# Differential attention in an encoder layer: a second plain fp32 quarter of the weights, and GpSimd work tied to VectorE's combinations

## The chip, the cores and the metric

The kernel runs on one core of one Trainium2 chip. The metric is the device time of one execution in microseconds. Three executions of the kernel before took 2710.55, 2710.61 and 2710.95 us; the median is 2710.61 us.

## The reference, cut to what matters

One encoder layer on x of 2048 positions by 1024 channels: RMS norm, an input projection, differential attention (4 heads) beside a gated linear recurrence (512 channels), an output projection, a gated feed-forward part with a short convolution, and a last RMS norm. All is fp32. The change touches the attention alone:

```
sc = einsum(q_block, k) * scale - slope[h] * |i - j|      # two score maps per head, c = 0, 1
p  = softmax(sc)
w  = p[c=0] - lam * p[c=1]                                # 128 queries x 2048 keys
o  = w @ v                                                # 128 queries x 128
o  = rms_norm(o, subln_g) * (1 - lambda_init)             # over the 128 columns
```

## The kernel before, in words

`phase1` makes q, k, v and the recurrence and leaves them in DRAM; `phase2` is the attention; `phase3` starts the output projection; then the feed-forward part runs. fp32 products are made either as one plain fp32 matmul, or by `mm3` (L79) as three fp32r matmuls of a high and a low part of each factor: high x high, high x low, low x high. `split` (L72) makes the parts: the high one is a copy to fp32r on ScalarE, the low one the fp32 difference, on VectorE or GpSimd as `lo_eng` says.

The attention works on 4 heads x 16 tiles of 128 queries, 64 steps, and two neighbouring tiles of a head form a pair. `step(n, cur)` (L550) writes the work of one step out by hand for five tiles at different ages. `manual_schedule` (L613) keeps this order on TensorE, VectorE, ScalarE and GpSimd up to the last of the 64 steps; the ten steps that drain the pipeline (L641) are ordered by the framework's planner. In the order of step n:

- `scores(0)` (L397): 12 fp32r matmuls give 1024 keys of both maps into the two buffers of PSUM tile `sc`; `softmax(1)` of the tile before (L415, ScalarE); `biased(0, 0)` and `biased(1, 0)` (L411, VectorE) add the position term and keep the running minimum. They empty `sc`, so `scores(1)` follows them.
- `transposed(0)` and `(1)` of the tile two steps back: 8 transposes of the weights on TensorE, and a copy of each four to SBUF on ScalarE (L442). Quarter 0 goes to `wTn`, plain fp32 for the value product; quarter 1 goes to `wf` and is split by `parts(1)`: high on ScalarE, low on GpSimd (L77, 128x512).
- `parts(2)` of the tile three steps back: the last two quarters (`wg`), high on ScalarE, low on GpSimd (128x1024).
- `values` (L460), two quarters of the product of the pair that is four steps old: in an even step quarters 0 and 1, in an odd one 2 and 3. Quarter 0 is 4 plain fp32 products (L465), each other quarter 12 matmuls of `mm3`. After quarter 3, ScalarE copies the product to `o` (L472) and GpSimd squares it (`osq`, L474).
- `ratio` and `combine(0)` of the tile before (L419 to L427, VectorE): `e0 += rc * e1` on 1024 keys, all in SBUF. The last small instruction of `ratio` (`rc`, L423) also reads two SBUF tensors.
- `scores(1)`, `biased(0, 1)`, `biased(1, 1)`, `transposed(2)` and `(3)`, `softmax(0)`, the second quarter of `values`, `combine(1)`.
- In even steps also the norm of older pairs: `norm_sums` on TensorE, `norm_scale` (VectorE `se`, then GpSimd `rr` and two rows `rb`), two steps later `norm_spread` on TensorE and `scaled` on VectorE (L500).

`sum_values` (L375) adds the two parts of v on GpSimd for the plain quarters, once per head. In the last head, after the odd steps 55, 57, 59 and 61 of 0 to 63, `load_out` (L512) splits a block of the output weights, `wo`: high on ScalarE, low on GpSimd (128x1024), each behind what the step has put on that engine.

Of the kernel before, what the change touches and what calls it, by code (L numbers as in the profile page):

```python
# [9 lines left out]
F32 = mybir.dt.float32  # L10
# [3 lines left out]
AF = mybir.ActivationFunctionType  # L14
ALU = mybir.AluOpType
# [3 lines left out]
P = 128  # L19
# [10 lines left out]
EPS = 1e-6  # L30
# [13 lines left out]
def encoder_layer(ctx, tc, x, w_qkr, w_v, w_out, w_up, w_down, w_a, w_x, par, lams, g_attn, g_ffn, g_fin, out):  # L44
    nc = tc.nc
    V, A, G, T = nc.vector, nc.scalar, nc.gpsimd, nc.tensor

    def pool_of(name, **kw):
        return tc.tile_pool(name=name, reuse_waits="tile", **kw)
# [17 lines left out]
    mhalf = const.tile([P, 4], F32, name="mhalf")  # L67
# [4 lines left out]
    def split(hi, lo, src, hi_eng=A, lo_eng=V):  # L72
        if hi_eng is A:
            A.activation(out=hi, in_=src, func=AF.Copy)  # L74
        else:
            hi_eng.tensor_copy(hi, src)
        lo_eng.tensor_tensor(out=lo, in0=src, in1=hi, op=ALU.subtract)  # L77

    def mm3(ps, lh, ll, rh, rl, first, last):  # L79
        T.matmul(ps, lh, rh, start=first, stop=False)  # L80
        T.matmul(ps, lh, rl, start=False, stop=False)  # L81
        T.matmul(ps, ll, rh, start=False, stop=last)  # L82
# [243 lines left out]
    def phase2(kp):  # L326
        es = ExitStack()
        hip = es.enter_context(pool_of("ah", bufs=2))
        sm = es.enter_context(pool_of("asm", bufs=3))
# [3 lines left out]
        tp_ = es.enter_context(pool_of("at", bufs=2))  # L333
# [4 lines left out]
        ps_t = es.enter_context(pool_of("ps_t", bufs=2, space=PSUM))  # L338
        ps_v = es.enter_context(pool_of("ps_v", bufs=1, space=PSUM))
        PQ = 2 * P  # L340
        NQ = 1

        ones = cp.tile([P, P], F32, name="ones")
        V.memset(ones, 1.0)
# [14 lines left out]
                        op0=ALU.mult)  # L359
# [15 lines left out]
        def sum_values(vs):  # L375
            vn = vp.tile([P, 4 * NQ, P], F32, name="vn", tag="vn")
            G.tensor_tensor(out=vn, in0=vs[0][:, 0:4 * NQ, :].bitcast(F32), in1=vs[1][:, 0:4 * NQ, :].bitcast(F32), op=ALU.add)
            vs.append(vn)
# [9 lines left out]
        class Tile:  # L388
# [35 lines left out]

            def combine(self, hf):
                e0, e1 = [e[:, hf * 1024:(hf + 1) * 1024] for e in self.e]
                V.scalar_tensor_tensor(out=e0, in0=e1, scalar=self.rc, in1=e0, op0=ALU.mult, op1=ALU.add)  # L427

            def transposed(self, i):

                tp = ps_t.tile([P, 4, P], F32, name="tp", tag="tp")
                for m in range(4):
                    T.transpose(tp[:, m, :], self.e[0][:, (4 * i + m) * P:(4 * i + m + 1) * P], ident)  # L433
                if i == 0:
                    dst = self.pair.wn[:, :, self.t % 2 * P:(self.t % 2 + 1) * P]
                elif i == 1:
                    dst = self.wf = tp_.tile([P, 4, P], F32, name="wf", tag="wf", bufs=1)
                else:
                    if i == 2:
                        self.wg = tp_.tile([P, 8, P], F32, name="wg", tag="wg")  # L440
                    dst = self.wg[:, (i - 2) * 4:(i - 1) * 4, :]
                A.activation(out=dst, in_=tp, func=AF.Copy)  # L442

            def parts(self, i):

                j = self.t % 2
                dst = (slice(None), slice(0, 4) if i == 1 else slice(4, 12), slice(j * P, (j + 1) * P))
                split(self.pair.wh[dst], self.pair.wl[dst], self.wf if i == 1 else self.wg, lo_eng=G)

        class Pair:  # L450


            def __init__(self, h, u, vs):
                self.h, self.u, self.vs = h, u, vs
                self.s0 = sm.tile([P, 2], F32, name="s0", tag="s0", bufs=8)
                self.wn = hip.tile([P, 4 * NQ, PQ], F32, name="wTn", tag="wTn")
                self.wh = hip.tile([P, NT - 4 * NQ, PQ], F32R, name="wTh", tag="wTh")
                self.wl = lop.tile([P, NT - 4 * NQ, PQ], F32R, name="wTl", tag="wTl")

            def values(self, part):  # L460
                if part == 0:
                    self.pv = ps_v.tile([P, PQ], F32, name="pv", tag="pv")
                for kt in range(part * 4, part * 4 + 4):
                    if part < NQ:
                        T.matmul(self.pv, self.vs[2][:, kt, :], self.wn[:, kt, :], start=kt == 0, stop=False)  # L465
                    else:
                        m = kt - 4 * NQ
                        mm3(self.pv, self.vs[0][:, kt, :], self.vs[1][:, kt, :], self.wh[:, m, :], self.wl[:, m, :],
                            kt == 0, kt == NT - 1)
                if part == 3:  # L470
                    self.o = sm.tile([P, PQ], F32, name="o", tag="o", bufs=3)
                    A.activation(out=self.o, in_=self.pv, func=AF.Copy)  # L472
                    self.sq = sm.tile([P, PQ], F32, name="osq", tag="osq", bufs=1)
                    G.tensor_tensor(out=self.sq, in0=self.o, in1=self.o, op=ALU.mult)  # L474
                    self.s2 = sm.tile([P, 2], F32, name="s2", tag="s2")
                    G.tensor_tensor(out=self.s2, in0=self.s0, in1=self.s0, op=ALU.mult)

            def norm_sums(self):
                self.ssp = nrm_ps[:, PQ:PQ + 4]
# [2 lines left out]

            def norm_scale(self):

                e0 = sm.tile([P, 2], F32, name="se", tag="se")
                V.scalar_tensor_tensor(out=e0, in0=self.s2, scalar=EPS * P, in1=self.ssp[:, 0:4:2], op0=ALU.mult, op1=ALU.add)
                r = sm.tile([P, 2], F32, name="rr", tag="rr")
                G.tensor_tensor(out=r, in0=e0, in1=mhalf[:, 0:2], op=ALU.pow)
                self.rb = sm.tile([P, 2, P], F32, name="rb", tag="rb", bufs=1)
                for j in range(2):  # L490
                    G.tensor_scalar(out=self.rb[:, j, :], in0=ones, scalar1=r[:, j:j + 1], scalar2=None, op0=ALU.mult)

            def norm_spread(self):

# [55 lines left out]
        def step(n, cur):  # L550

            b1 = tiles[n - 1] if 0 <= n - 1 < last else None
            b2 = tiles[n - 2] if 0 <= n - 2 < last else None
            pair = lambda lag: pairs[(n - lag) // 2] if n >= lag and (n - lag) // 2 < len(pairs) else None
            pv, nrm, fin = pair(4), pair(6), pair(8)
            if n % 2:
                nrm = fin = None
            b3 = tiles[n - 3] if 0 <= n - 3 < last else None
            if cur:
                cur.scores(0)  # L560
            if b1:
                b1.softmax(1)
            if cur:
                cur.biased(0, 0)
                cur.biased(1, 0)
            if b2:
                b2.transposed(0)
                b2.transposed(1)
                b2.parts(1)
            if b3:  # L570
                b3.parts(2)
            if pv:
                pv.values(n % 2 * 2)
            if fin:
                fin.norm_spread()
            if b1:
                b1.ratio()
                b1.combine(0)
            if cur:
                cur.scores(1)  # L580
                cur.biased(0, 1)
                cur.biased(1, 1)
            if b2:
                b2.transposed(2)
                b2.transposed(3)
            if cur:
                cur.softmax(0)
            if pv:
                pv.values(n % 2 * 2 + 1)
            if nrm:  # L590
                nrm.norm_sums()
            if b1:
                b1.combine(1)
            if fin:
                fin.scaled()
            if nrm:
                nrm.norm_scale()

        ordered = {mybir.EngineType.PE, mybir.EngineType.DVE, mybir.EngineType.Activation, mybir.EngineType.Pool}
        ks, vs = load_head(0)  # L600
# [40 lines left out]
        while n < last + 10:  # L641
            step(n, None)
            early.run(n - last)
            if n == last + 1:
                load_two((0, 1), (1, 2))
            if n == last + 4:
                load_two((2, 0), (3, 3))
            n += 1
# [511 lines left out]
    kp_stack = ExitStack()  # L1160
    kp = kp_stack.enter_context(pool_of("kp", bufs=2, side="right"))
    wo, x0 = phase2(kp)
    sl = Slots()
    sl.add(ctx.enter_context(pool_of("ba", bufs=1)), [f"b{i}" for i in range(9)])
# [73 lines left out]
```

## Time and profile before

| of the profiled execution | |
|---|---|
| its own time, and its span | 2708.57 us, 2706.6 us |
| PE busy (matmuls) | 2629.2 us, 97% of the span |
| PEld busy (weight loads) | 2143.8 us, 79% |
| DVE (VectorE) | 1841.4 us, 68% |
| ACT (ScalarE) | 1306.4 us, 48% |
| POOL (GpSimd) | 543.5 us, 20% |
| mean granted clock of TensorE | 0.987 of 2.4 GHz |

The span runs from the first to the last instruction. Matmuls are pipelined and their ends are modelled, so the start of the next weight load (PEld) tells better than PE's busy time when a group of matmuls has made room. The attention's 64 steps lie between about 526 and 1100 us. An "idle before" in a row is the engine's empty time just before the instruction, with what ended it.

### The profile page before, as it was taken

The numbers are of one execution on the slowest core, as the hardware profiler recorded it, in microseconds if no ns is written. First come the engines' busy times: TensorE is split into PE (matmuls) and PEld (weight loads), VectorE is DVE, ScalarE is ACT, GpSimd is POOL, SyncE is SP. The second block draws the span as 40 slices with busy tenths as digits, with TensorE's granted clock in tenths as the row PEclk, the third lists the DMA queues.
The fourth block names the chain that finished last, engine by engine and source line by source line (L and its number), as shares of the span: only waits on it lengthen the run. The fifth ranks groups of instructions, "written<-read, shape, count | busy, mean of one in ns | idle before, by whom it ended". The sixth has DMA issues, their size and how long they took to land.

```text
span 2706.6 us, 33137 instructions
## 1 busy us (share of the span) xinstructions
PE 2629.2 (97%) x13168; PEld 2143.8 (79%) x13168; DVE 1841.4 (68%) x2248; ACT 1306.4 (48%) x1625; POOL 543.5 (20%) x435
## 2 busy tenths in 40 slices
PE   8999999899999999999899999979999999999998
PEld 6878778678888887787688888858888878888887
DVE  5453553699999999634588888898888882233333
ACT  4343543588888888523344444444444451121222
POOL 1013313347676666600000000000000000000000
PEclk9999999899999999999999999989999999999999
DMA  6421221411111001434422222312122254344443
GB/s 192 125 86 57 80 86 63 165 47 55 56 42 69 18 23 38 142 109 153 143 86 78 86 78 86 125 63 94 70 94 70 94 189 145 118 178 169 150 164 131
DMA packets 122379, 271.89 MB, mean 100 GB/s; under 512 B 15792, under 2 KB 52144, under 8 KB 115056
## 3 DMA queue, kind: packets, MB, share of 16 engines
q1 hardware_dynamic: 120016, 263.63, 28.3%
q0 software_dynamic: 1632, 4.46, 0.5%
q8 instruction: 103, 1.69, 0.3%
q10 hardware_dynamic: 576, 1.69, 0.2%
q14 instruction: 52, 0.43, 0.1%
HBM read 187.94 MB, written 81.79 MB: 100 GB/s over the span
## 4 chain that ended last, share of the span: by engine, by line
PE 88%; DVE 4%; issue 2%; ACT 2%; POOL 2%; DMA 1%; SPq 0%; POOLq 0%; DVEq 0%; ACTq 0%
PE q L864 30%; PE sc L407 7%; PE pd L82 6%; PE pd L80 6%; PE pd L81 6%; PE ps L82 5%; PE ps L81 5%; PE ps L80 4%; PE tp L433 4%; PE po L82 2%; PE po L81 2%; PE po L80 2%; PE pv L465 2%; PE pv L81 2%; PE pv L80 2%
## 5 line engine op out<-in xcount | busy, mean ns | idle before, releaser
L90 POOL TENSOR_TENSOR r<-ss,mhalf 128x1 f32<-128x1 f32 x48 | 27.5, 574 | 1633.3 <-DVE ss L88 1633.3
L77 DVE TENSOR_TENSOR dal<-dal,dah 128x2048 fp32r<-128x2048 f32 (+1 forms) x47 | 99.2, 2110 | 274.5 <-ACT dah L74 274.5
L416 ACT ACTIVATE e<-e,mn 128x2048 f32<-128x2048 f32 x128 | 256.2, 2007 | 16.2 <-DVE mn L411 16.2
L407 PE MATMUL sc<-ks,qt 64*128 64x512 f32 x1536 | 234.1, 421 | 16.0 <-DVE mn L411 11.6
L957 DVE SCALAR_TENSOR_TENSOR acc<-u,prm,acc 128x1023 f32<-128x1023 f32 (+1 forms) x176 | 226.0, 1284 | 7.6 <-ACT acc L949 1.4
L832 ACT ACTIVATE wg<-sw 128x1024 fp32r<-128x1024 f32 x88 | 93.4, 1061 | 285.2 <-PE q L864 281.5
L74 ACT ACTIVATE dah<-dal 128x2048 fp32r<-128x2048 f32 (+1 forms) x47 | 83.2, 1770 | 304.7 <-DMA dal<-a_d 301.7
L876 DVE TENSOR_TENSOR u<-q,u 128x512 f32<-128x512 f32 x220 | 151.6, 689 | 94.0 <-PE q L864 89.1
L427 DVE SCALAR_TENSOR_TENSOR e<-e,rc,e 128x1024 f32<-128x1024 f32 x128 | 212.6, 1662 | 2.3
L82 PE MATMUL ps<-hT_hi,wl 128*128 128x512 f32 x512 | 199.6, 390 | 0.0
L81 PE MATMUL ps<-hT_lo,wh 128*128 128x512 f32 x512 | 199.5, 390 | 0.0
L80 PE MATMUL ps<-hT_hi,wh 128*128 128x512 f32 x512 | 199.4, 390 | 0.0
L407 PEld LDWEIGHTS sc<-ks,qt 64*128 64x128 f32 x1536 | 148.3, 190 | 61.0 <-DVE mn L411 20.0
L411 DVE CUSTOM_DVE_ANT_0 e<-sc,strip,mn 128x1024 f32<-128x1024 f32 x128 | 159.1, 1281 | 17.1 <-PE sc L407 14.3
L949 ACT ACTIVATE acc<-u,prm 128x1023 f32<-128x1023 f32 (+1 forms) x88 | 109.4, 1243 | 104.8 <-issue 51.2
L411 DVE CUSTOM_DVE_ANT_0 e<-sc,strip 128x1024 f32<-128x1024 f32 x128 | 150.9, 1213 | 9.2 <-PE sc L407 9.2
L77 POOL TENSOR_TENSOR wTl<-wg,wTh 128x1024 fp32r<-128x1024 f32 x64 | 156.4, 2443 | 0.0
L77 POOL TENSOR_TENSOR wTl<-wf,wTh 128x512 fp32r<-128x512 f32 x64 | 126.4, 1976 | 112.9 <-ACT wTh L74 110.4
L433 PEld LDWEIGHTS tp<-ident,e 128*128 128x128 f32 x1024 | 111.7, 142 | 46.3 <-ACT wTh L74 19.8
L433 PE MATMUL tp<-ident,e 128*128 128x128 f32 x1024 | 142.0, 282 | 0.0
L864 PE MATMUL q<-b4r,wg 128*128 128x512 f32 x352 | 117.5, 395 | 7.4 <-ACT u L888 7.4
L864 PE MATMUL q<-b12r,wg 128*128 128x512 f32 x352 | 119.7, 401 | 4.8 <-ACT u L888 4.8
(348 smaller groups left out, 6913.2 us busy)
## 6 DMA issues: line engine op xcount, KB each, us to landing
wr<-in_w_up_dram SPq DMA_DIRECT2D x88, 512.0 KB, 4.3
dal<-a_d SPq DMA_DIRECT2D x39, 1024.0 KB, 4.9
a_d<-acc SPq DMA_DIRECT2D x66, 256.0 KB, 2.0
xt<-in_x_dram SPq DMA_DIRECT2D x30, 512.0 KB, 5.0
ws<-in_w_qkr_dram SPq DMA_DIRECT2D x16, 512.0 KB, 3.4
qt<-q_d SPq DMA_DIRECT2D x32, 256.0 KB, 3.2
ks<-k_d SPq DMA_DIRECT2D x8, 1024.0 KB, 7.7
vt<-v_d SPq DMA_DIRECT2D x8, 1024.0 KB, 7.3
```

Source lines behind the costliest of these rows:

```text
L77: lo_eng.tensor_tensor(out=lo, in0=src, in1=hi, op=ALU.subtract)
L80: T.matmul(ps, lh, rh, start=first, stop=False)
L81: T.matmul(ps, lh, rl, start=False, stop=False)
L82: T.matmul(ps, ll, rh, start=False, stop=last)
L407: T.matmul(self.sc[c][:, n * CH:(n + 1) * CH], l[rows, q], r[rows, kk], start=i == 0, stop=i == 2)
L411: V.tensor_tensor_reduce(out=self.e[c][:, hf * 1024:(hf + 1) * 1024], in0=self.sc[c], in1=strip[:, off:off + 1024], scale=SLOPES[self.h], ...
L416: A.activation(out=self.e[c], in_=self.e[c], func=AF.Exp, scale=-1.0, bias=self.mn[:, 2 * c + 1:2 * c + 2], accum_out=self.s[c])
L427: V.scalar_tensor_tensor(out=e0, in0=e1, scalar=self.rc, in1=e0, op0=ALU.mult, op1=ALU.add)
L433: T.transpose(tp[:, m, :], self.e[0][:, (4 * i + m) * P:(4 * i + m + 1) * P], ident)
L864: T.matmul(ps, l, r[:, k, :], start=new is not None and k == 0 and n == 0, stop=k == 3 and n == 2, skip_group_check=True)
L876: V.tensor_tensor(out=out, in0=a, in1=b_, op=ALU.add)
L957: V.scalar_tensor_tensor(out=acc[:, 0:n], in0=u[:, o + tap:o + tap + n], scalar=prm[:, C_FW + 3 * m + tap:C_FW + 3 * m + tap + 1], in1=acc ...
```

## The change: what it does

`NQ` goes from 1 to 2: quarters 0 and 1 are both plain fp32 in the value product, `wTn` and `vn` hold 8 blocks, `wTh` and `wTl` 8 instead of 12. `wf`, its high copy and its low part are gone. `parts(2)` becomes `high` (ScalarE), now issued one step earlier, after `softmax(0)`, and `low` (GpSimd), still in the step after that. `squares` moves from behind the copy of `o` to the next even step, `norm_rows` from the end of that step to the odd step after. `after` adds waits for VectorE: `low` for `combine(1)` of the step before, `squares` and the first `rb` row for `combine(0)` of their own step. `load_out` and `sum_values` get no such wait.

```diff
-        NQ = 1
+        NQ = 2
@@ class Tile
-                if i == 0:
-                    dst = self.pair.wn[:, :, self.t % 2 * P:(self.t % 2 + 1) * P]
-                elif i == 1:
-                    dst = self.wf = tp_.tile([P, 4, P], F32, name="wf", tag="wf", bufs=1)
+                if i < NQ:
+                    dst = self.pair.wn[:, 4 * i:4 * i + 4, self.t % 2 * P:(self.t % 2 + 1) * P]
...
-            def parts(self, i):
+            def high(self):
                 j = self.t % 2
-                dst = (slice(None), slice(0, 4) if i == 1 else slice(4, 12), slice(j * P, (j + 1) * P))
-                split(self.pair.wh[dst], self.pair.wl[dst], self.wf if i == 1 else self.wg, lo_eng=G)
+                self.dst = (slice(None), slice(None), slice(j * P, (j + 1) * P))
+                A.activation(out=self.pair.wh[self.dst], in_=self.wg, func=AF.Copy)
+
+            def low(self):
+                return G.tensor_tensor(out=self.pair.wl[self.dst], in0=self.wg, in1=self.pair.wh[self.dst], op=ALU.subtract)
@@ class Pair: values() loses osq and s2, norm_scale() loses rr and rb; they become
+            def squares(self):
+                self.sq = sm.tile([P, PQ], F32, name="osq", tag="osq", bufs=1)
+                self.s2 = sm.tile([P, 2], F32, name="s2", tag="s2")
+                G.tensor_tensor(out=self.s2, in0=self.s0, in1=self.s0, op=ALU.mult)
+                return G.tensor_tensor(out=self.sq, in0=self.o, in1=self.o, op=ALU.mult)
+            def norm_rows(self):
+                r = sm.tile([P, 2], F32, name="rr", tag="rr")
+                G.tensor_tensor(out=r, in0=self.se, in1=mhalf[:, 0:2], op=ALU.pow)
...
@@ def step(n, cur)
-            pv, nrm, fin = pair(4), pair(6), pair(8)
+            pv, nrm, fin, row = pair(4), pair(6), pair(8), pair(7)
...
+            if b3:
+                after(b3.low(), "second")
             if b2:
                 b2.transposed(0)
                 b2.transposed(1)
-                b2.parts(1)
-            if b3:
-                b3.parts(2)
...
                 b1.ratio()
-                b1.combine(0)
+                marks["first"] = b1.combine(0)
...
+            if nrm:
+                after(nrm.squares(), "first")
+            if row:
+                after(row.norm_rows()[0], "first")
...
                 cur.softmax(0)
+            if b2:
+                b2.high()
...
-                b1.combine(1)
+                marks["second"] = b1.combine(1)
...
+        def after(ins, mark):
+            if mark in marks:
+                tc.add_manual_dep(ins.ins, marks[mark].ins.name,
+                                  mybir.DependencyInfo(mybir.DependencyClass.Sync, mybir.DependencyReason.SCHED_ONLY),
+                                  reason="shared access to SBUF")
```

## Rows read from the trace of the kernel before

**Rows 1.** Stretches: length, busy PE, PEld, DVE, ACT, POOL; clock, DMA share, GB/s.

```profile
690.00:1010.00 320.00, 320.00 (x2414) 268.61 (x2412) 309.65 (x475) 282.27 (x384) 220.93 (x166) 1.00 0.13 43
...
1030.00:1055.00 25.00, 22.27 (x144) 18.08 (x143) 20.50 (x31) 17.77 (x25) 14.15 (x13) 0.86 0.10 32
...
1095.00:1140.00 45.00, 41.01 (x242) 35.57 (x241) 22.34 (x27) 19.08 (x28) 29.65 (x26) 0.96 0.44 151
```

**Rows 2.** Groups by line, 690 to 1010 us: busy, mean ns; idle before.

```profile
L427 DVE SCALAR_TENSOR_TENSOR e<-e,rc,e 128x1024 f32<-128x1024 f32 x74 | 122.2, 1652 | 1.3
...
L77 POOL TENSOR_TENSOR wTl<-wg,wTh 128x1024 fp32r<-128x1024 f32 x37 | 89.5, 2418 | 0.0
```

**Rows 3.** Timeline of TensorE's weight loads in one pair: start, us, instruction.

```profile
900.65 1.23 PEld L407 LDWEIGHTS sc<-ks,qt 64*128 64x128 f32 x12
...
903.07 0.19 PEld L80 LDWEIGHTS pv<-wTh,vt 128*128 128x128 f32 x1
...
904.50 0.53 PEld L481 LDWEIGHTS nrm_ps<-ones,osq 128*128 128x128 f32 x4
...
905.04 1.23 PEld L407 LDWEIGHTS sc<-ks,qt 64*128 64x128 f32 x12
...
909.10 1.46 PEld L407 LDWEIGHTS sc<-ks,qt 64*128 64x128 f32 x12
...
911.75 0.19 PEld L80 LDWEIGHTS pv<-wTh,vt 128*128 128x128 f32 x1
...
913.39 1.23 PEld L407 LDWEIGHTS sc<-ks,qt 64*128 64x128 f32 x12
...
915.82 1.60 PEld L465 LDWEIGHTS pv<-wTn,vn 128*128 128x128 f32 x8
...
917.44 0.63 PEld L497 LDWEIGHTS nrm_ps<-ident,rb 128*128 128x128 f32 x4
...
918.19 0.99 PEld L407 LDWEIGHTS sc<-ks,qt 64*128 64x128 f32 x10
```

**Rows 4.** Timeline of the same pair on VectorE, ScalarE and GpSimd.

```profile
902.35 1.28 DVE L411 CUSTOM_DVE_ANT_0 e<-sc,strip,mn 128x1024 f32<-128x1024 f32 x1 [0.41 <-PE sc L407]
...
903.97 2.01 ACT L416 ACTIVATE e<-e,mn 128x2048 f32<-128x2048 f32 x1
...
912.04 2.44 POOL L77 TENSOR_TENSOR wTl<-wg,wTh 128x1024 fp32r<-128x1024 f32 x1
...
913.26 2.30 DVE L427 SCALAR_TENSOR_TENSOR e<-e,rc,e 128x1024 f32<-128x1024 f32 x1
```

**Rows 5.** Timeline around the first block of output weights, step 55 into 56.

```profile
1020.10 1.06 ACT L74 ACTIVATE wo<-wos 128x1024 fp32r<-128x1024 f32 x1
...
1021.33 2.37 POOL L77 TENSOR_TENSOR wo<-wos,wo 128x1024 fp32r<-128x1024 f32 x1
...
1023.18 0.16 DVE L422 RECIPROCAL rc<-s 128x1 f32<-128x1 f32 x1 [0.15 <-ACT e L416]
```

**Rows 6.** Timeline of VectorE and GpSimd, steps 57 to 63, first row of some steps.

```profile
1030.02 1.21 DVE L411 CUSTOM_DVE_ANT_0 e<-sc,strip 128x1024 f32<-128x1024 f32 x1
...
1032.49 1.35 DVE L423 SCALAR_TENSOR_TENSOR rc<-rc,s,nlam 128x1 f32<-128x1 f32 x1
...
1033.78 2.39 POOL L77 TENSOR_TENSOR wTl<-wg,wTh 128x1024 fp32r<-128x1024 f32 x1
...
1033.87 3.38 DVE L427 SCALAR_TENSOR_TENSOR e<-e,rc,e 128x1024 f32<-128x1024 f32 x1
...
1053.41 1.23 DVE L411 CUSTOM_DVE_ANT_0 e<-sc,strip 128x1024 f32<-128x1024 f32 x1 [0.23 <-PE sc L407]
...
1074.02 2.28 DVE L427 SCALAR_TENSOR_TENSOR e<-e,rc,e 128x1024 f32<-128x1024 f32 x1
...
1075.17 3.38 POOL L77 TENSOR_TENSOR wTl<-wg,wTh 128x1024 fp32r<-128x1024 f32 x1
...
1089.63 1.22 DVE L411 CUSTOM_DVE_ANT_0 e<-sc,strip 128x1024 f32<-128x1024 f32 x1
```

More of the change, by code (lines that the diff above doesn't have):

```diff
@@ L426, in combine @@
                 e0, e1 = [e[:, hf * 1024:(hf + 1) * 1024] for e in self.e]
-                V.scalar_tensor_tensor(out=e0, in0=e1, scalar=self.rc, in1=e0, op0=ALU.mult, op1=ALU.add)
+                return V.scalar_tensor_tensor(out=e0, in0=e1, scalar=self.rc, in1=e0, op0=ALU.mult, op1=ALU.add)
             def transposed(self, i):
@@ L433, in transposed @@
                     T.transpose(tp[:, m, :], self.e[0][:, (4 * i + m) * P:(4 * i + m + 1) * P], ident)
-                if i == 0:
-                    dst = self.pair.wn[:, :, self.t % 2 * P:(self.t % 2 + 1) * P]
-                elif i == 1:
-                    dst = self.wf = tp_.tile([P, 4, P], F32, name="wf", tag="wf", bufs=1)
-                else:
-                    if i == 2:
-                        self.wg = tp_.tile([P, 8, P], F32, name="wg", tag="wg")
-                    dst = self.wg[:, (i - 2) * 4:(i - 1) * 4, :]
+                if i < NQ:
+                    dst = self.pair.wn[:, 4 * i:4 * i + 4, self.t % 2 * P:(self.t % 2 + 1) * P]
+                else:
+                    if i == NQ:
+                        self.wg = tp_.tile([P, 4 * (4 - NQ), P], F32, name="wg", tag="wg")
+                    dst = self.wg[:, (i - NQ) * 4:(i - NQ + 1) * 4, :]
                 A.activation(out=dst, in_=tp, func=AF.Copy)
-            def parts(self, i):
+            def high(self):
                 j = self.t % 2
-                dst = (slice(None), slice(0, 4) if i == 1 else slice(4, 12), slice(j * P, (j + 1) * P))
-                split(self.pair.wh[dst], self.pair.wl[dst], self.wf if i == 1 else self.wg, lo_eng=G)
+                self.dst = (slice(None), slice(None), slice(j * P, (j + 1) * P))
+                A.activation(out=self.pair.wh[self.dst], in_=self.wg, func=AF.Copy)
+            def low(self):
+                return G.tensor_tensor(out=self.pair.wl[self.dst], in0=self.wg, in1=self.pair.wh[self.dst], op=ALU.subtract)
         class Pair:
@@ L472, in values @@
                     A.activation(out=self.o, in_=self.pv, func=AF.Copy)
[L473 to L476, printed above, removed]
+            def squares(self):
[3 more added lines that the diff above has]
+                return G.tensor_tensor(out=self.sq, in0=self.o, in1=self.o, op=ALU.mult)
             def norm_sums(self):
@@ L483, in norm_scale @@
             def norm_scale(self):
-                e0 = sm.tile([P, 2], F32, name="se", tag="se")
-                V.scalar_tensor_tensor(out=e0, in0=self.s2, scalar=EPS * P, in1=self.ssp[:, 0:4:2], op0=ALU.mult, op1=ALU.add)
+                self.se = sm.tile([P, 2], F32, name="se", tag="se")
+                V.scalar_tensor_tensor(out=self.se, in0=self.s2, scalar=EPS * P, in1=self.ssp[:, 0:4:2], op0=ALU.mult, op1=ALU.add)
+            def norm_rows(self):
                 r = sm.tile([P, 2], F32, name="rr", tag="rr")
-                G.tensor_tensor(out=r, in0=e0, in1=mhalf[:, 0:2], op=ALU.pow)
+                G.tensor_tensor(out=r, in0=self.se, in1=mhalf[:, 0:2], op=ALU.pow)
                 self.rb = sm.tile([P, 2, P], F32, name="rb", tag="rb", bufs=1)
-                for j in range(2):
-                    G.tensor_scalar(out=self.rb[:, j, :], in0=ones, scalar1=r[:, j:j + 1], scalar2=None, op0=ALU.mult)
+                return [G.tensor_scalar(out=self.rb[:, j, :], in0=ones, scalar1=r[:, j:j + 1], scalar2=None, op0=ALU.mult)
+                        for j in range(2)]
             def norm_spread(self):
@@ L554, in step @@
             pair = lambda lag: pairs[(n - lag) // 2] if n >= lag and (n - lag) // 2 < len(pairs) else None
-            pv, nrm, fin = pair(4), pair(6), pair(8)
+            pv, nrm, fin, row = pair(4), pair(6), pair(8), pair(7)
             if n % 2:
                 nrm = fin = None
+            else:
+                row = None
             b3 = tiles[n - 3] if 0 <= n - 3 < last else None
@@ L597, in step @@
                 nrm.norm_scale()
+        marks = {}
+        def after(ins, mark):
[3 more added lines that the diff above has]
+                                  reason="shared access to SBUF")
         ordered = {mybir.EngineType.PE, mybir.EngineType.DVE, mybir.EngineType.Activation, mybir.EngineType.Pool}
```

## The prediction, before the result was known

> **What bounds the kernel now.** The page's slices put the attention where PE, DVE and ACT are all high, so I read it first by stretches [rows 1]: from 690 to 1010 us PE is covered without a hole, at granted clock 1.00, DVE is busy 309.65 of 320 us and GpSimd 220.93. Two engines are near full, so the groups come next [rows 2]: VectorE's `combine` takes 1652 ns on the mean, 74 times. The timeline shows why. One of them runs 2.30 us: it starts at 913.26 while GpSimd's low part, started at 912.04, runs to 914.48, and it ends 1.08 us after that [rows 4]. So a combine asked for while GpSimd subtracts waits for the end of that instruction. A clean one needs those 1.08 us and a start-up of some 0.2 that the wait hid (an estimate), so the mean loss is between 1652 - 1280 and 1652 - 1080 ns, 0.4 to 0.6 us, about 1 us a step.
>
> Whether that loss sets the time is read on TensorE's weight loads [rows 3]. A pair of steps lasts 918.19 - 900.65 = 17.54 us. I cut it at the starts of the four `sc` groups: 900.65 to 905.04 (4.39 us, second half of the even step), 905.04 to 913.39 (8.35, the odd step), 913.39 to 918.19 (4.80, first half of the next even step). In the even parts the groups follow each other without a stall: each `sc` group loads in 1.23 us. In the odd step one `sc` group (909.10) loads in 1.46 us, 0.23 more: its second matmul waits for `biased(1, 0)`. So TensorE itself needs 17.54 - 0.23 = 17.31 us of the 17.54. VectorE's lost 2 us a pair are nearly all hidden behind TensorE: in the even step VectorE waits 0.41 us for scores after its combine [rows 4]. The whole attention before its end is TensorE's.
>
> **The change, part by part.**
>
> *The second plain quarter* goes to TensorE, 4 products for 12, once a pair. A three-part quarter takes 904.50 - 903.07 = 1.43 us, a plain one 917.44 - 915.82 = 1.62 [rows 3]. That is +0.19 us where it stands, in the second half of the even step, which has no stall to give.
>
> *Freed from GpSimd's lock,* VectorE starts the odd step's first `biased` earlier. In the odd step the chain is: scores to `biased` 1.70 us (900.65 to 902.35 [rows 3, 4]), two `biased`, scores again. From `sc` at 905.04 TensorE's own work reaches the next `sc` 4.06 us later (909.10); from there 1.70, two `biased` of 1.21 with the gap left in (2.42) and 0.13 to TensorE make 4.25. Sum 8.31 instead of 8.35, a gain of 0.04. Pair: 17.54 + 0.19 - 0.04 = 17.69. Steps 8 to 55 hold 24 pairs: 24 x 0.15 = **+3.6 us**. The ends: no stall at all in the odd step gives 17.50, -1.0 us; a `biased` 0.15 late once a pair gives +7.
>
> *Steps 2 to 7* have no norm work, so VectorE's waits weigh there. At most 6 x 1 = 6 us go; TensorE gets 2 x 0.19 more. I take **-1**, nearer to the pair's result than to the full lock loss.
>
> *The high copy before `softmax(1)`.* ScalarE's copy of quarter 1 goes and hides nothing. The other is now between `softmax(0)` and `softmax(1)`. `softmax(0)` starts 903.97 - 900.65 = 3.32 us after the second `sc` group; with 2.0 for it, 0.96 for the copy (1.06 on a like row, 1020.10 [rows 5], less the overlap of neighbours), 2.15 for `softmax(1)` and its sum, `ratio` can start 8.4 us after that `sc`, 8.7 in odd steps with the copy of `o`. VectorE wants it at 4.58 + 1.70 + 2.28 = 8.56 after an even step and 8.0 after an odd one, but the `biased` behind that combine waits until 4.25 + 4.80 + 1.70 = 10.75 for scores, and `ratio` and combine need 1.65. So it is hidden, with 0.3 us to spare. If this cover is gone, each 0.1 costs up to 3 us in all; that is the third rival.
>
> *The waits on marks.* `low` waits for `combine(1)`, but its high copy ends 0.9 us later, so that copy lets it go. It runs 2.42 us [rows 2] and ends about when `ratio` ends, 0.1 to 0.2 ahead of `combine(0)`. Queued behind it on GpSimd are the norm rows and squares; TensorE needs the rows 8 us and the squares 1.5 us later. Cost 0, between -0 and the third rival.
>
> *The four `wo` blocks.* Here lies the price. Today's row: high part at W = 1020.10 on ScalarE, low part on GpSimd from W + 1.23 for 2.37 us, to W + 3.60; `ratio` starts at W + 3.08 [rows 5], its `rc` at about W + 3.28, so it is held to W + 3.60, and the combine asks at W + 3.65. GpSimd's next instruction today waits for ScalarE. After the change it is `low` of the even step, whose mark and high copy have long passed; it follows at once, as at 1033.78, where `rc` was held 1.35 us and the combine behind it, asked for 0.09 us after GpSimd had begun, ran 3.38 [rows 6]. So combine would end at W + 3.56 + 2.40 + 1.08 = W + 7.04. W is 3.32 + 2.0 + 0.96 + 0.26 = 6.54 after the second `sc` group, so VectorE reaches `biased(0, 1)` at 13.5 us, which scores allow at 10.75. With 2.42 + 0.13 to the next `sc` at 16.0, and TensorE free at 9.0 + 4.58 = 13.58, an event costs 2.4 us. What more it may cost is seen in the one event of today: steps 57 and 58 take 1053.41 - 1030.02 = 23.39, 5.85 above a pair, though VectorE was held for only (1.35 - 0.2) + (3.38 - 1.3) = 3.2: TensorE stood still, and the granted clock of 1030 to 1055 is 0.86 [rows 1, 6], a part of it at the lower of the two levels, 1.2 GHz. That is 2.6 us more. Four events cost 9.6 us if the clock stays, 20 if it falls each time; the idle time is somewhat shorter than today's, so I take half: 14.7. Against it stands what the stretch loses now: steps 57 to 62 take 1089.63 - 1030.02 = 59.61, three pairs are 52.62, so 7.0 us go. Net **+7.7**.
>
> The row at 913.26 is a lock for the whole instruction, not a slower pace. The Trainium skill says so too (SBUF — State Buffer, section "SBUF: two separate sides"): the read and write port that VectorE and GpSimd share is given to whichever starts first, and the other is fully blocked. It speaks against the change, since a wait moves such a collision and does not shorten it. Were the port shared at half speed instead, a combine would be late by about 1.2 us, an event cost about 0.8, and the sum below end near 2707; rows and rule both speak for the lock.
>
> *The drain.* From 1095 to 1140 TensorE is idle 4.0 us and GpSimd busy 29.65 of 45 [rows 1]. The low parts of quarter 1 go. At most 4 us are to be had, the planner may lose 2: **-2**.
>
> *`sum_values`* gets twice the elements, three times beside the steps; its 2.5 us delay a `combine(1)` by about 1.3, which the odd step's slack to 10.75 hides: 0.
>
> Sum: 3.6 - 1 + 7.7 - 2 = +8.3. The profiled execution, 2708.57 us, would take 2716.9; the median of the runs stands 2.04 above it, and its forecast is 2710.61 + 8.3 = **2719 us**.
>
> **The rivals.** A change under 0.2%, 5.4 us, can't be told from none.
>
> 1. *VectorE gets the port first in the `wo` steps.* A combine that asks while GpSimd is still in the instruction before wins: at 1074.02 one asked 1.1 us before GpSimd's end, and GpSimd's next, dispatched at 1075.17, took 3.38 [rows 6]. It decides by whether `rc` is through before W + 3.60; it misses by 0.3 us. Then `low` runs beside `biased`, an event costs only the later `softmax(1)`, 0.35, and the stretch gains 7.0 - 1.4 = 5.6: 3.6 - 1 - 5.6 - 2 = -5.0, **2706**. For it: a few tenths decide. Against: ScalarE's `wo` copy sets both starts, so the gap is the same each time.
> 2. *TensorE's seams close.* Between a quarter of three parts (911.75 + 1.43) and `sc` at 913.39 lie 0.21 us, twice in the odd step [rows 3]. If that is VectorE's doing, 0.42 of a pair goes: 24 x (0.15 - 0.42) = -6.5; with the first rival's stretch -15: **2696**. Against: 909.10 starts no sooner though its first matmul had its data.
> 3. *The hidden chain comes out.* If ScalarE's copy, or `rc` held by `low`, makes each pair 0.4 us longer than I think, 24 x 0.4 = +9.6 on top: **2728**. For it: the spare 0.3 us. Against: the even step waits 0.41 for scores even now.
> 4. *The marks do nothing,* since the high copy comes later anyway: true by my sum, and it changes no time; it is part of every case.
>
> **How the numbers follow.** Forecast 0.43 (slower 0.36, no change 0.07), first rival 0.34 (half faster, half no change), second 0.08 (faster), third 0.15 (slower 0.14). Faster 0.25, within 0.2% 0.25, slower 0.50. The forecast's own range is 2712 (clock stays, drain at its best) to 2727 (clock falls each time). The range, 2702 to 2727, takes in the first rival with 4 us below it and leaves out the second and most of the third.
>
> **What would show it.** Right: pairs of 17.6 to 17.8 us; a plain quarter of 1.62 in both places; combine below 1.4 us except after each `wo` low part, there 3.4, four times, with `sc` held behind it. Wrong: combine short in those steps; pairs under 17.5; `rc` waiting for `softmax(1)` with TensorE idle in every step.

## The result: slower by 18 us, and where they lie

The changed kernel takes 2729.03 us (median; 2725.50 to 2730.07 in four runs) against 2710.78 us for the kernel before (2710.55 to 2711.78): a ratio of 1.0064, 95% interval 1.0047 to 1.0082. Slower was forecast, with 2719 us and a range that ends at 2727; the measured time lies beyond it.

The stretches first: busy time by engine in three windows of the trace, the first two as in [rows 1], in the changed kernel (columns as there).

```profile
690.00:1010.00 320.00, 320.00 (x2294) 271.79 (x2292) 285.56 (x464) 254.16 (x340) 137.32 (x128) 1.00 0.13 43
1030.00:1055.00 25.00, 23.59 (x158) 19.17 (x155) 21.28 (x32) 17.18 (x23) 11.98 (x11) 0.93 0.16 48
1055.00:1095.00 40.00, 37.16 (x247) 29.68 (x248) 34.45 (x51) 29.21 (x39) 21.54 (x16) 0.96 0.10 34
```

In the middle of the attention VectorE falls from 309.65 to 285.56 us and GpSimd from 220.93 to 137.32, as the change sets out to do, and TensorE is full as before: less work on engines that were not the bound. The groups of the same stretch, to set beside [rows 2]:

```profile
L427 DVE SCALAR_TENSOR_TENSOR e<-e,rc,e 128x1024 f32<-128x1024 f32 x72 | 94.6, 1314 | 1.3
...
L449 POOL TENSOR_TENSOR wTl<-wg,wTh 128x1024 fp32r<-128x1024 f32 x36 | 86.9, 2413 | 136.1 <-PE sc L407 78.4 <-ACT wTh L446 55.3 <-DVE e L427 2.5
```

A combine now takes 1314 ns on the mean, not 1652. Where the time went is seen by cutting each profiled execution at the first `biased` of steps 0, 8, 56 and 63 (starts of that instruction in the timeline; the pair is step 18 to step 54, divided by 18). All profiles of this study, in us:

| kernel | to step 0 | 0 to 8 | 8 to 56 | 56 to 63 | after 63 | pair | median time |
|---|---|---|---|---|---|---|---|
| before | 528.8 | 71.1 | 420.8 | 69.0 | 1617.0 | 17.54 | 2710.8 |
| changed | 534.8 | 71.4 | 428.9 | 76.5 | 1616.7 | 17.87 | 2729.0 |
| 1 quarter alone | 532.3 | 71.4 | 427.1 | 63.1 | 1618.6 | 17.79 | 2712.1 |
| 2 no marks | 531.9 | 72.9 | 428.9 | 76.5 | 1620.0 | 17.87 | 2726.3 |
| 3 `wo` on VectorE | 529.6 | 73.0 | 433.0 | 76.2 | 1617.6 | 17.87 | 2736.4 |
| 4 plain quarter last | 530.3 | 71.3 | 423.7 | 76.3 | 1613.9 | 17.66 | 2716.8 |
| 5 `wo` early | 528.7 | 71.4 | 430.2 | 70.2 | 1617.7 | 17.87 | 2725.3 |
| 6 quarter alone, last | 531.6 | 76.6 | 460.3 | 72.6 | 1618.9 | 19.18 | 2761.8 |
| 7 early and last | 529.8 | 71.5 | 425.0 | 71.9 | 1615.1 | 17.66 | 2716.7 |
| 8 `o` first | 529.7 | 72.8 | 427.1 | 78.0 | 1618.2 | 17.80 | 2727.5 (one run) |
| 9 before, `wo` early | 530.3 | 71.9 | 420.8 | 63.0 | 1617.5 | 17.53 | 2703.6 |
| 10 the same, drain ordered | 531.9 | 71.2 | 421.6 | 63.2 | 1618.3 | 17.56 | 2707.7 |
| 11 early, last, drain ordered | 532.3 | 72.8 | 425.0 | 63.5 | 1616.7 | 17.66 | 2708.9 |
| 12 before again | 532.9 | 71.1 | 420.9 | 66.1 | 1615.4 | 17.53 | 2708.3 (one run) |

One profile is one execution: run 5's is 5.4 us below the median of its runs, run 3's 5.2 below, run 2's 5.8 above. Stretches can be set side by side, but they don't add up to a difference of medians.

The changed profile's span is 21.6 us longer: 6.0 ahead of step 0, 0.3 in the fill, 8.1 in the steady pairs, 7.5 in steps 56 to 62, -0.3 behind. The 6.0 are not all the change's: the unchanged kernel's second profile (run 12) has 4.1 of them.

**The steady pair**, on TensorE's weight loads, to set beside [rows 3]:

```profile
895.41 1.23 PEld L407 LDWEIGHTS sc<-ks,qt 64*128 64x128 f32 x12
...
897.83 1.60 PEld L466 LDWEIGHTS pv<-wTn,vn 128*128 128x128 f32 x8
899.45 0.63 PEld L484 LDWEIGHTS nrm_ps<-ones,osq 128*128 128x128 f32 x4
900.09 1.23 PEld L407 LDWEIGHTS sc<-ks,qt 64*128 64x128 f32 x12
...
904.15 1.29 PEld L407 LDWEIGHTS sc<-ks,qt 64*128 64x128 f32 x12
...
908.27 1.37 PEld L407 LDWEIGHTS sc<-ks,qt 64*128 64x128 f32 x12
910.01 0.86 PEld L433 LDWEIGHTS tp<-ident,e 128*128 128x128 f32 x8 [0.37 <-ACT e L416]
910.90 1.59 PEld L466 LDWEIGHTS pv<-wTn,vn 128*128 128x128 f32 x8
912.52 0.63 PEld L502 LDWEIGHTS nrm_ps<-ident,rb 128*128 128x128 f32 x4
913.27 0.76 PEld L407 LDWEIGHTS sc<-ks,qt 64*128 64x128 f32 x8
```

Second half of the even step 4.68 us (before 4.39), odd step 8.18 (8.35), first half of the even step 5.00 (4.80). In the first of these the plain quarter takes 1.62 us as forecast, and the norm sums behind it 0.64 where they took 0.54. In the last one 0.14 is the stall that moved here from the odd step (`sc` at 908.27 loads in 1.37), and the transposes take 0.89 to the plain quarter where 0.83 is usual (914.99 to 915.82 before).

**The `wo` blocks.** ScalarE, GpSimd, VectorE and the weight loads behind the second block:

```profile
1057.35 1.06 ACT L74 ACTIVATE wo<-wos 128x1024 fp32r<-128x1024 f32 x1
...
1058.49 2.39 POOL L77 TENSOR_TENSOR wo<-wos,wo 128x1024 fp32r<-128x1024 f32 x1 [5.61 <-ACT wo L74]
...
1060.62 0.28 DVE L423 SCALAR_TENSOR_TENSOR rc<-rc,s,nlam 128x1 f32<-128x1 f32 x1
1060.82 2.39 POOL L449 TENSOR_TENSOR wTl<-wg,wTh 128x1024 fp32r<-128x1024 f32 x1
1060.93 3.36 DVE L427 SCALAR_TENSOR_TENSOR e<-e,rc,e 128x1024 f32<-128x1024 f32 x1
...
1065.11 0.52 PEld L484 LDWEIGHTS nrm_ps<-ones,osq 128*128 128x128 f32 x4 [1.20 <-POOL osq L479]
...
1066.76 1.23 PEld L407 LDWEIGHTS sc<-ks,qt 64*128 64x128 f32 x11 [0.93 <-DVE mn L411]
```

This is the forecast's collision to a tenth: `rc` ends with the block's low part (at 1060.9), the next low part has started by then, and the combine asked for at 1060.93 ends 7 us after the block's high copy began. It happens behind all four blocks; steps 56, 58, 60 and 62 take 12.4, 11.7, 12.7 and 13.6 us where the steady even step takes 9.69. The granted clock is 0.93 and 0.96 in the stretches around them. Ahead of the scores TensorE also waits 1.20 us for `osq`, the squares that GpSimd now makes behind its low part.

### The profile page after: what moved, and what is told of

It reads as the page before. It is cut to its first block, busy times and chain, and to the rows that moved or that the text cites. A ratio compares the mean times of both kernels' runs of the same rounds, so it can differ in the third digit from the quotient of the medians.

```text
span 2728.2 us, 32751 instructions
## 1 busy us (share of the span) xinstructions
PE 2643.1 (97%) x13040; PEld 2156.4 (79%) x13040; DVE 1813.4 (66%) x2248; ACT 1267.7 (46%) x1561; POOL 411.5 (15%) x371
## 4 chain that ended last, share of the span: by engine, by line
PE 72%; DVE 3%; issue 1%; ACT 1%; POOL 1%; DMA 1%; SPq 0%; POOLq 0%; ACTq 0%; DVEq 0%
PE q L885 30%; PE sc L407 7%; PE pd L82 6%; PE pd L80 6%; PE pd L81 6%; PE tp L433 4%; PE pv L466 3%; PE po L82 2%; PE po L81 2%; PE po L80 2%; PE pv L81 1%; PE pv L80 1%; PE pv L82 1%; DVE e L411 1%; PE tp L739 0%
## 5 line engine op out<-in xcount | busy, mean ns | idle before, releaser
L407 PEld LDWEIGHTS sc<-ks,qt 64*128 64x128 f32 x1536 | 158.0, 191 | 55.8 <-DVE mn L411 21.2
L427 DVE SCALAR_TENSOR_TENSOR e<-e,rc,e 128x1024 f32<-128x1024 f32 x128 | 177.6, 1388 | 2.3
L411 DVE CUSTOM_DVE_ANT_0 e<-sc,strip,mn 128x1024 f32<-128x1024 f32 x128 | 159.2, 1281 | 15.6 <-PE sc L407 11.9
L466 PE MATMUL pv<-wTn,vn 128*128 128x256 f32 x512 | 123.2, 383 | 0.1
```

The costliest lines, as they stand in the source:

```text
L407: T.matmul(self.sc[c][:, n * CH:(n + 1) * CH], l[rows, q], r[rows, kk], start=i == 0, stop=i == 2)
L411: V.tensor_tensor_reduce(out=self.e[c][:, hf * 1024:(hf + 1) * 1024], in0=self.sc[c], in1=strip[:, off:off + 1024], scale=SLOPES[self.h], ...
L427: return V.scalar_tensor_tensor(out=e0, in0=e1, scalar=self.rc, in1=e0, op0=ALU.mult, op1=ALU.add)
```

## The experiments

**1. The quarter alone**: the kernel before with `NQ = 2`; high and low parts, squares and norm rows stay where they were.

```diff
-        NQ = 1
+        NQ = 2
...
-                b2.parts(1)
```

> The kernel before with the second plain quarter alone: no waits on marks, high and low parts, squares and norm rows where they were. My theory: the steady pair of steps costs 0.29 us more on TensorE because of the quarter (0.19 for 4 plain products in place of 12, 0.10 because the norm sums load 0.10 us slower behind plain products), so pairs of 17.8 us, about 7 us in all; at the weight blocks of the last head the one long stall of before (7 us) may go, as GpSimd has less to do: 2711 to 2718 us. Rival, that the waits and moves make the change slow: pairs stay at 17.5 us and the time is 2711 or less.

Measured: 2712.05 us, ratio 1.0009 (1.0000 to 1.0018); pairs of 17.79, both as expected. The quarter costs 6.2 us in the steady pairs without any of the moves. Steps 56 to 62 take 63.1 us, no more than seven steady steps (4 x 9.61 + 3 x 8.18 = 63.0): the stall of before is gone, and with it 5.9 us. The rows behind a block show why:

```profile
1031.73 2.37 POOL L77 TENSOR_TENSOR wo<-wos,wo 128x1024 fp32r<-128x1024 f32 x1 [0.18 <-ACT wo L74]
...
1034.15 1.29 DVE L427 SCALAR_TENSOR_TENSOR e<-e,rc,e 128x1024 f32<-128x1024 f32 x1
...
1035.63 2.38 POOL L77 TENSOR_TENSOR wTl<-wg,wTh 128x1024 fp32r<-128x1024 f32 x1 [1.53 <-ACT wTh L74]
```

GpSimd's next low part waits 1.53 us for its high copy, and the combine goes first. The changed kernel takes 17 us more than this one; 13.4 lie in steps 56 to 62 and 1.9 in steps 8 to 55, both of the moves. That it is the early high copy, which lets `low` follow the `wo` part at once, is read from these rows; no run moved that copy alone.

**2. No marks**: `after` adds nothing.

```diff
-            if mark in marks:
+            if False:
```

> The changed kernel without the three waits for VectorE's combinations (all moves stay). My theory: the low part waits longer for its high copy than for the mark, so pairs stay at 17.87 us and the time within 3 us of 2729. Rival, that the waits cost time: pairs shorter by 0.1 us or more, 2726 or less. Rival, that the waits save time: combinations of 2 us and more come back on VectorE and the time goes above 2732.

Measured: 2726.3 us (2725.84 to 2732.09), as expected; pairs of 17.87 and steps 56 to 62 of 76.5 us, as in the changed kernel. The marks move neither. They do act a little beside the path:

```profile
L427 DVE SCALAR_TENSOR_TENSOR e<-e,rc,e 128x1024 f32<-128x1024 f32 x72 | 98.3, 1366 | 1.3
...
L495 POOL TENSOR_SCALAR rb<-ones,rr 128x128 f32<-128x128 f32 x36 | 32.7, 918 | 1.8
```

From 690 to 1010 us a combine takes 1366 ns where the changed kernel has 1314, and GpSimd's `rb` rows 918 where it has 607.

**3. `wo` low parts on VectorE**, in the changed kernel.

```diff
-                    load_out(t // 2 + 1, t // 2 - 3, G, raw)
+                    load_out(t // 2 + 1, t // 2 - 3, V, raw)
```

> The changed kernel with the low parts of the four output-weight blocks on VectorE, not GpSimd. My theory: the four combinations of 3.4 us behind them go, steps 56 to 62, now 13 us above the steady ones, lose 10 to 13 us: 2716 to 2719. Rival, that ScalarE's copy of each block ahead of the second softmax is what delays these steps: at most 4 us less, 2725 or more.

Measured: 2736.36 us, a miss of both. The timeline at the first block:

```profile
1053.27 2.38 POOL L449 TENSOR_TENSOR wTl<-wg,wTh 128x1024 fp32r<-128x1024 f32 x1 [3.47 <-ACT wTh L446]
...
1054.44 2.29 DVE L77 TENSOR_TENSOR wo<-wos,wo 128x1024 fp32r<-128x1024 f32 x1 [2.29 <-ACT wo L74]
...
1056.65 1.21 DVE L411 CUSTOM_DVE_ANT_0 e<-sc,strip 128x1024 f32<-128x1024 f32 x1
...
1057.92 0.18 PEld L407 LDWEIGHTS sc<-ks,qt 64*128 64x128 f32 x1 [2.17 <-DVE mn L411]
```

The combine behind the block is short here, but VectorE stands 2.29 us for ScalarE's high copy, then its subtraction is held by `low` until 1055.65, and the scores wait for it. Steps 55, 57, 59 and 61 take 12.2 to 12.3 us where 8.18 is steady; the first of them lies in the table's stretch 8 to 56. A wait at the head of VectorE's queue costs no less than the lock that it avoids.

**4. The plain quarter last**: quarters in the order 0, 2, 3, 1, in the changed kernel.

```diff
-                for kt in range(part * 4, part * 4 + 4):
-                    if part < NQ:
+                q = (0, 2, 3, 1)[part]
+                for kt in range(q * 4, q * 4 + 4):
+                    if q < NQ:
```

> The changed kernel with the quarters of the value product in the order 0, 2, 3, 1: the second plain quarter stands in the second half of the odd step, where TensorE waits for VectorE, and the norm sums again behind a three-part quarter. My theory: even halves of 4.4 and 4.9 us, odd step 8.3, pair 17.5 to 17.6 and 24 to 28 x 0.3 = 7 to 9 us less: 2720 to 2722. Rival, that the odd step has no room for it either: pair 17.8 or more, 2727 or more.

Measured: 2716.79 us, ratio 1.0029 (1.0018 to 1.0040). The weight loads:

```profile
898.14 1.60 PEld L467 LDWEIGHTS pv<-wTn,vn 128*128 128x128 f32 x8
900.07 1.23 PEld L407 LDWEIGHTS sc<-ks,qt 64*128 64x128 f32 x12 [0.33 <-DVE mn L411]
...
904.86 1.22 PEld L407 LDWEIGHTS sc<-ks,qt 64*128 64x128 f32 x12
...
908.70 0.53 PEld L485 LDWEIGHTS nrm_ps<-ones,osq 128*128 128x128 f32 x4
909.25 1.23 PEld L407 LDWEIGHTS sc<-ks,qt 64*128 64x128 f32 x12
```

Behind a three-part quarter the norm sums take 0.55 again, and that half of the even step 4.39 (904.86 to 909.25). But the odd step grows from 8.18 to 8.48: it does not hide the quarter. From its first load to the scores behind it the plain quarter takes 1.93 us (898.14 to 900.07), a three-part one 1.64 ([rows 3], 911.75 to 913.39). That is 0.29 more, the same as in the even step with the norm sums between (2.26 against 1.97). The row at 900.07 names VectorE for the 0.33, but VectorE had let go by 899.85, and in run 11 the same gap behind the quarter is put down to no wait, with the first buffer of `sc` free since 1044.78:

```profile
899.77 0.08 DVE L411 DVE_READ_ACCUMULATOR2_ANT mn<- 128x1 f32 x1
```

```profile
1043.47 1.60 PEld L467 LDWEIGHTS pv<-wTn,vn 128*128 128x128 f32 x8
1045.39 0.18 PEld L407 LDWEIGHTS sc<-ks,qt 64*128 64x128 f32 x1 [0.33 <-issue]
```

So the 0.33 is TensorE's own seam. What the new place wins is in the first half of the even step, 4.79 us and not 5.00: TensorE is longer at work in the odd step, so VectorE's stall of 0.14 is over when the scores come, and the wait of 0.06 for `o` (run 8) is gone too. Pair 17.66, 5 us less in steps 8 to 56: I had expected 0.3 us a pair, and from hiding the quarter. 7 more come from elsewhere: 4.5 ahead of step 0, which varies, and 2.8 after step 63, which I can't place.

**5. `wo` early**: in the changed kernel the block's high copy moves to the end of the even step before (and its load one step further up), so that GpSimd can do the low part right behind the odd step's norm rows.

```diff
+                if h == NH - 1 and t in (6, 8, 10, 12):
+                    both = kp.tile([P, 2, D], F32R, name="wo", tag=f"kp{t // 2 - 3}")
+                    A.activation(out=both[:, 0, :], in_=raw, func=AF.Copy)
                 if h == NH - 1 and t in (7, 9, 11, 13):
-                    load_out(t // 2 + 1, t // 2 - 3, G, raw)
+                    G.tensor_tensor(out=both[:, 1, :], in0=raw, in1=both[:, 0, :], op=ALU.subtract)
```

> The changed kernel with each output-weight block's high part on ScalarE one step earlier (end of the even step), so that its low part on GpSimd can run straight behind the norm rows of the odd step and not ahead of the even step's low part. My theory: the combinations of 3.4 us go, because GpSimd's low part of the even step no longer starts just when a block's low part ends; a second combination may be 1.3 us late once a block, which the odd step hides as it does after a head's sum of values. Steps 56 to 62 fall from 76.5 us to 63 to 66: 2715 to 2719 us. Rival, that these blocks cost the same wherever GpSimd does them: 73 us or more, 2725 or more.

Measured: 2725.34 us (2719.99 to 2725.67). Steps 56 to 61 take 8.9 and 9.4 us by turns, 18.3 a pair where the changed kernel's first such pair took 21.5: the combines of 3.4 us are gone (2.5 remains, once a block), and a block costs 0.45. But step 62 takes 15.2, and the whole stretch 70.2, between my figure and the rival's; the median time is the rival's. What step 62 runs into, the edit brings on:

```profile
1089.02 1.15 POOL L76 CAST ch<-cl 128x1024 fp32r<-128x1024 f32 x1 [4.77 <-DMA cl<-cat_l]
1090.25 2.37 POOL L77 TENSOR_TENSOR cl<-cl,ch 128x1024 fp32r<-128x1024 f32 x1
1092.59 3.33 POOL L449 TENSOR_TENSOR wTl<-wg,wTh 128x1024 fp32r<-128x1024 f32 x1
```

The planner has put GpSimd's first split of the drain ahead of the last low parts, and it waits for its load, which needs the buffer that the last `wo` block was loaded into (`wos`, free when its low part ends at 1084.25).

**6. The quarter alone, last**: runs 1 and 4 together.

> The quarter alone (first run, 2712 us, pairs of 17.79) with the quarters in the order 0, 2, 3, 1. My theory: as in the changed kernel the pair falls by 0.2 us, to about 17.6, 24 to 28 x 0.2 = 5 to 6 us: 2706 to 2708, below the kernel before. Rival, that without the early high copy the odd step has other waits (GpSimd's low part ends later there) and does not take the quarter: 17.8 and 2712.

Measured: 2761.75 us, pairs of 19.18, a miss of both figures, though the wait is the rival's. Run 1 has the late low part, and now quarter 2 is wanted one place of `values`, half a step, sooner. From 690 to 1010 us:

```profile
L427 DVE SCALAR_TENSOR_TENSOR e<-e,rc,e 128x1024 f32<-128x1024 f32 x66 | 104.0, 1575 | 1.2
L77 POOL TENSOR_TENSOR wTl<-wg,wTh 128x1024 fp32r<-128x1024 f32 x34 | 94.2, 2770 | 72.1 <-ACT wTh L74 72.1
L81 PEld LDWEIGHTS pv<-wTl,vt 128*128 128x128 f32 x136 | 25.7, 189 | 9.1 <-POOL wTl L77 9.1
```

TensorE waits 9.1 us for low parts and, more, for VectorE, whose combine is held by GpSimd in every second pair (the 19.8 takes in some gaps of 0.33 as in run 4):

```profile
PEld sc L407 <- DVE mn L411: 19.8, 25, 1.0
```

```profile
889.36 2.38 POOL L77 TENSOR_TENSOR wTl<-wg,wTh 128x1024 fp32r<-128x1024 f32 x1 [1.54 <-ACT wTh L74]
889.39 3.43 DVE L427 SCALAR_TENSOR_TENSOR e<-e,rc,e 128x1024 f32<-128x1024 f32 x1
```

I had looked at the place in TensorE's order and not at when its operand is ready. Run 4 has the same order and the moves, and neither wait; by the code it is the early high copy, of the moves, that lets the low part start earlier.

**7. Early and last**: runs 4 and 5 together.

> The changed kernel with both: early high parts of the blocks and the order 0, 2, 3, 1. If the two costs are separate, pairs of 17.66 and steps 56 to 62 of 62 to 65 us: 2729 - 12 - 12 = 2705 us, within 3. If they hang together, less than 20 us are won: 2709 or more.

Measured: 2716.67 us (ratio 1.0025, 1.0016 to 1.0034), a miss of my theory; the rival's figure came, but not because the two costs hang together: pairs of 17.66 and steps 56 to 61 of 8.6 and 9.7 are as expected, and step 62 takes 17.0 for the same early split.

**8. `o` first**: the high copy behind ScalarE's copy of the product.

```diff
-            if b2:
-                b2.high()
             if pv:
                 pv.values(n % 2 * 2 + 1)
+            if b2:
+                b2.high()
```

> The changed kernel with ScalarE's copy of the product o ahead of the high copy. My theory: the product of the next pair waits 0.06 us in PSUM's one buffer for that copy, so the first half of the even step falls from 5.00 to 4.94 us and the pair from 17.87 to 17.81. Rival, that the 0.06 is TensorE's own: 17.87 stays.

Measured: one run, 2727.49 us; pair 17.80. The first half of the even step falls to 4.95:

```profile
903.30 1.39 PEld L407 LDWEIGHTS sc<-ks,qt 64*128 64x128 f32 x12
905.05 0.86 PEld L433 LDWEIGHTS tp<-ident,e 128*128 128x128 f32 x8 [0.37 <-ACT o L473]
905.88 1.60 PEld L466 LDWEIGHTS pv<-wTn,vn 128*128 128x128 f32 x8
...
908.25 1.22 PEld L407 LDWEIGHTS sc<-ks,qt 64*128 64x128 f32 x12
```

0.83 from the transposes to the quarter, not 0.89: the 0.06 was the wait for `o`. The single time can't tell a gain of 2 us; the rows do.

**9. Before, `wo` early**: the edit of run 5 in the kernel before.

> The kernel before with the early high parts of the output-weight blocks alone. My theory: the long stall of steps 57 and 58 comes from a block's low part on GpSimd that starts late and pushes the next low parts into the combinations; with its high part ready it ends 1 us earlier against the rest and the stretch of steps 56 to 62 falls from 69 us to 62 to 64, if the split that follows the last step is not pulled ahead of a low part: 2703 to 2706. Rival, that it is again pulled ahead as in the fifth run: 5 us of it come back, 2709 or more.

Measured: 2703.60 us against 2709.39 beside it, ratio 0.9980 (0.9971 to 0.9989), faster than both kernels and as expected. Steps 56 to 62 take 63.0 us (69.0 in the first profile of before, 66.1 in run 12's), pairs 17.53. The split is pulled ahead of a low part here too, but waits only 1.30 us for its load, and step 62 takes 9.31.

**10 and 11. The drain's first split held behind step 63**, in run 9's kernel and in run 7's.

```diff
-        manual.close()
-
         early = EarlyOut()
+        manual.close()
```

> As the run before, and GpSimd's first split of the drain (of the recurrence's output) is held behind the last of the 64 steps by the written order. My theory: no wait for that load in step 62, steps 56 to 62 at 62 to 63 us and the drain not longer: 2702 to 2705. Rival, that the drain gives it back, since its first product starts later: 2708 or more.

> The changed kernel with order 0, 2, 3, 1, early high parts and the first split of the drain held behind the last step. My theory: step 62 falls from 17.0 us to 9 to 10, so 2716.7 - 7 = 2709 to 2711, about the kernel before, since each pair still costs 0.12 us more than before. Rival: the drain gives it back and it stays above 2714.

Measured: 2707.72 us (ratio 0.9994, 0.9985 to 1.0003) and 2708.93 us (1.0003, 0.9994 to 1.0012). Run 11's step 62 falls from 17.0 to 8.6 us, as expected, and the change ends level with the kernel before, with the pair 0.12 us dearer and the `wo` stretch 5.5 us cheaper (2.6 against run 12). In run 10 the edit has nothing to mend; its median is 4 us above run 9's, between my two figures, and the stretches don't say by what (1.5 ahead of step 0, 0.8 in the pairs, 0.8 after step 63).

**12. Before again**, unchanged.

> The kernel before, unchanged, for a second profile. The changed kernel's profile has 6 us more than the one of before ahead of the first step, in code that the change leaves alone. My theory: that stretch varies from run to run by some us in any kernel, so here it may lie anywhere from 0 to 6 us above the first profile, with pairs of 17.54 again. Rival, that the change causes it: 0 here.

Measured: 2708.27 us in one run, pairs of 17.53; 532.9 us to step 0 against 528.8, as expected. Steps 56 to 62 take 66.1 us and not 69.0, so that stretch varies as well. The second profile of the kernel before and the changed kernel's have the same row near the start, at the norm of an input tile:

```profile
28.96 2.38 POOL L77 TENSOR_TENSOR wl<-ws,wh 128x1024 fp32r<-128x1024 f32 x1
29.03 3.39 DVE L127 SCALAR_TENSOR_TENSOR xt<-xt,r,g_b 128x1024 f32<-128x1024 f32 x1 [0.44 <-POOL r L90]
```

```profile
29.05 3.40 DVE L127 SCALAR_TENSOR_TENSOR xt<-xt,r,g_b 128x1024 f32<-128x1024 f32 x1 [0.44 <-POOL r L90]
```

In the first profile of before it is GpSimd's subtraction there that waits:

```profile
27.42 3.48 POOL L77 TENSOR_TENSOR wl<-ws,wh 128x1024 fp32r<-128x1024 f32 x1
```

Whichever asks first holds the other. The projections end 3.1 us later in the two profiles in which VectorE is held (last product at 524.5, not 521.4). Over all 14 profiles, step 0 starts at 531.6 to 534.8 us in the six in which VectorE is held there, and at 528.7 to 532.3 in the eight in which GpSimd is. That the meeting is the cause was not tried, nor what tips it; and the whole time does not follow it, 2708.27 us here against 2708.57.

## Why the prediction fell short

- *What bounds the kernel* was right. TensorE is full before and after; freeing 24 us of VectorE and 84 us of GpSimd in 320 us won nothing.
- *The second plain quarter* is the step that failed. "+0.19 us where it stands" was the length of its own loads; what follows a plain quarter is also 0.10 us later (the norm sums load in 0.64 and not 0.54; in run 4 the scores start after 1.93 and not 1.64), so the term is 0.29. [rows 3] had a hint: `norm_spread`, behind the plain quarter 0, loads in 0.63 us, the norm sums in 0.53. I bounded the term with a stall in the odd step and never with the seam behind it.
- *The odd step.* 8.31 with its last stall was forecast for the chain; measured 8.18 and 0.14 of stall. Right.
- *The high copy before `softmax(1)`* does not hold up `ratio`, as forecast (its spare time is 0.4 us by its own figures, not 0.3). What I put at nothing is that it delays `o`, and with it the one PSUM buffer of the product: 0.06 of the pair, and 0.07 to 0.08 with what follows (run 8).
- *The pair* now comes out: TensorE's own 17.31 and 0.29 for the quarter make 17.60; stalls of 0.06 (`sc` at 904.15) and 0.14, and 0.06 for `o`, make 17.86. Forecast was 17.69, measured 17.87, just outside the sign of 17.6 to 17.8. The increase is 0.33 and not 0.15: 8.1 us and not 3.6 in 24 pairs. The upper end that I gave (+7) was too low as well.
- *The marks* do nothing for the time, as the fourth rival said (run 2).
- *The `wo` blocks*: +7.7 forecast, +7.5 measured, by the mechanism named, four combines of 3.4 us; the closeness is part luck. Above seven steady steps of its own kernel the stretch takes 13.2 us (14.7 forecast), and before it took 7.4 (7.0 forecast): 5.8 more; the other 1.7 are the dearer steps themselves, which the forecast did not count from step 56 on. Beside run 12's 66.1 the stretch is 10.4 longer. Run 5 removes the collisions by moving the block's high copy and low part. The first rival (VectorE goes first) did not come.
- *Fill* -1, measured +0.3; *drain* -2, measured -0.3 from step 63 on. GpSimd's work in the drain did go, 34.92 to 23.79 of the 50 us from step 63 on, but TensorE stands idle 6.48 of them in place of 4.83: I took the time that GpSimd loses for time that TensorE gains. What holds TensorE there was not followed up.

```profile
1089.63:1139.63 50.00, 45.17 (x273) 38.94 (x274) 27.26 (x35) 22.95 (x34) 34.92 (x29) 0.97 0.40 137
```

```profile
1111.51:1161.51 50.00, 43.52 (x250) 36.51 (x249) 26.36 (x40) 21.55 (x32) 23.79 (x22) 0.97 0.39 129
```

- Two sums of the forecast don't follow from its terms. A lock at half speed would cost 1.5 us an event by its figures, not 0.8, and end near 2710, not 2707. The upper end, "clock falls each time", gives 2724 with the terms for fill and drain; 2727 needs both at nothing.
- The stretches from step 0 on together give 15.6 us of 18.3, where 8.3 was forecast. Of the 10 us between, the pairs are 4.5, fill and drain 3.0, the blocks -0.2. The other 2.7 are of the size by which the stretch ahead of step 0 and the drain vary from profile to profile, and are not assigned.

## What to carry to other kernels

Where one engine is full, an exchange of its work for another's is decided by its own instruction starts: price the seam behind the new group, not only the group. A wait tied to one piece of GpSimd's work protects nothing if an untied piece stands in front of it and the tied one can follow at once; moving the untied piece (run 9) is worth more here than the wait. Before moving a product earlier in one engine's order, look up when its operands are ready on the others. And compare two kernels' windows from the same step, not from the same time.

## What the runs showed of the hardware

What stands behind four plain fp32 products of 256 columns is 0.10 us later than behind the 12 fp32r products of a three-part quarter, beyond the 0.19 that their own loads take more: 0.29 in all to the next scores, with the norm sums between and without. The lock between VectorE and GpSimd is asked for even by an instruction of one column: `rc` takes 0.22 us alone, and 1.35 when GpSimd subtracts [rows 6].

```profile
917.95 0.22 DVE L423 SCALAR_TENSOR_TENSOR rc<-rc,s,nlam 128x1 f32<-128x1 f32 x1
```

A combine that already waits when GpSimd's instruction ends goes next, and GpSimd's next one takes 3.38 us (1074.02 and 1075.17 in [rows 6]). One asked for 0.05 us after that end (1060.93 behind the second `wo` block) finds GpSimd's next instruction in front of it and takes 3.36 us, where one that nothing holds takes 1.28.
